# The first projection block worked in two halves of tokens, with its split weights kept in other buffers

## The chip, the cores and the metric

The kernel runs on one core of a Trainium2 chip. The metric is the device time of one execution in microseconds (us). The engines are named as in the profile: PE is the matrix engine, PEld its weight loads, DVE the vector engine, ACT the scalar engine, POOL the third one, SP the engine that issues most of the loads (its queue is SPq).

## The reference

One decoder layer over 512 tokens of width 2048. An RMS norm of x, one wide input projection, two token mixers fed from slices of that projection (an mLSTM and a gated delta rule), an output projection, a gated merge, and a last norm:

```python
D_MODEL = 2048; SEQ = 512
def _hybrid_layer(h, norm_w, w_in, ...):
    u = _rmsnorm(h, norm_w)                    # 512 x 2048
    proj = jnp.matmul(u, w_in.astype(jnp.float32))
    (ml_q, ml_k, ml_v, ml_o, ml_z, ml_i, ml_f,
     dn_qkv, dn_z, dn_b, dn_a, gate_a, gate_b) = jnp.split(proj, idx, axis=-1)
    h_a = mlstm(ml_q, ml_k, ml_v, ml_i, ml_f) ...
    h_b = gated_delta(dn_qkv, dn_b, dn_a) ...
    return jax.nn.sigmoid(gate_a) * (h_a @ w_out[:2048]) + jax.nn.sigmoid(gate_b) * (h_b @ w_out[2048:])
```

The change touches only the norm of x and the first 256 columns of the projection (a quarter of those of ml_q), with what runs beside them.

## The kernel before, in words

All matrices are f32. To multiply them at the faster rate of a reduced format, each operand is split into a high part (a cast to that format, `split_hi`, L135, on ACT) and a low part (the difference, `split_lo`, L138, on DVE); a product is then three matmuls: high by high, high by low, low by high (L261 to L263).

The start of the program runs like this. x lies as four tiles of 128 tokens by 2048 (`xts`), each loaded in two halves of 1024 columns by SP (L274). For each tile, ACT sums the squares of the first half (L301) and DVE those of the second (L303); two tiny operations and a power on POOL (L305, L306, L308) give the factor of each token; `scale_x` scales the first half on DVE (L294) and the second on ACT (L296). Then `make_u(kt)` makes slice kt (of 16) of the normalised input, tokens along the free axis: PE transposes the four tiles' 128 columns into one PSUM tile `put` (L317), ACT writes the high part `uh` (L318, times the norm weights `normc`), DVE the low part `ul` (L319).

The projection's weights come in pieces of 256 rows by 256 columns (two slices of k) in an order fixed by the list `plan`: `load_raw` issues a load on SP (L176) into one of four buffers `wr`, `split_next` splits it into `wh` and `wl` (four buffers each), and `prepare` keeps raw loads four pieces ahead and splits three ahead of the piece in use. A raw buffer comes free when its low part is written.

The first block, `proj_cm(ML_Q, before=first_block)`, runs over the 16 slices, two to a weight piece. Before a piece's products stand the transposes for the slices two ahead (UA = 2), and for later slices the products of the small gate columns (`gate_products`, L328 and L329, into `pgr`, eight slices behind). The products of one piece are 2 x 2 x 3 = 12 matmuls, each with a 128 x 128 weight part as the stationary operand and 512 tokens as the moving one. `first_block` also issues the loads of the gate columns (`wg`, two pieces, L333 and L334) and of small parameters, splits `wg` into `wgp`, and turns the convolution taps (`turn_taps`).

Behind the block come three more such blocks of q and k, then the main part, which works by sums of operand halves. Those sums are kept, split, in two large buffers `suh` and `sul` (L241); `u_sums` (L372 on) writes them once the first block is over:

```python
suh, sul = (sap.tile([P, KH, 3, HP], F32R, tag=f"su{n}", name=f"su{n}") for n in "hl")
```

KH is 8 and HP is 256. PE's instructions stand in the order in which they are written; those of the other engines are put in order by a scheduler, with hints of priority (`tc.high_priority`) and of place (`tc.issue_after`, `behind`). `tick()` moves side work on by one step.

Of the kernel before, what the change touches and what calls it, by code (L numbers as in the profile page):

```python
# [8 lines left out]
F32 = mybir.dt.float32  # L9
F32R = mybir.dt.float32r  # L10
AF = mybir.ActivationFunctionType
ALU = mybir.AluOpType
# [3 lines left out]
P = 128  # L16
# [39 lines left out]
def hybrid_body(  # L56
# [42 lines left out]
    def load_norms(tp, psp):  # L99
        nr = tp.tile([16, P], F32, tag="prow", name="nrow")  # L100
        nc.sync.dma_start(nr, norm_w.rearrange("(a p) -> a p", p=P))
        pt = psp.tile([P, 16], F32, tag="wk", name="pprm")
        T.transpose(pt, nr, ident[0:16, 0:16])
        V.tensor_copy(normc[:, 0:16], pt)

    def load_params(tp):
        nr = tp.tile([17, P], F32, tag="prow2", name="nrow2")
        nc.sync.dma_start(nr[0:16, :], ml_norm_w.rearrange("(a p) -> a p", p=P))
        nc.sync.dma_start(nr[16:17, :], dn_norm_w.rearrange("(a p) -> a p", p=P))
        cv = dn_conv_w.rearrange("j (a p) -> (j a) p", p=P)  # L110
# [29 lines left out]
    def behind(eng):  # L140

        return tc.issue_after(newest[eng])
# [17 lines left out]
    def load_raw():  # L160
        kind, c, k = plan[len(raws)]
        if kind == "m":

            qk = w_in[k * P:(k + KP) * P, ML_Q:ML_V].rearrange("(k p) (a n) -> p k a n", p=P, a=2)[:, :, :, c * P:(c + 1) * P]
            src, nk, n = None, KP, NB
        elif kind == "i":
            src, nk, n = w_in[k * P:(k + KP) * P, c:c + NB], KP, NB
        else:
            src, nk, n = w_out[k * P:(k + 1) * P, c:c + NO], 1, NO
        with tc.high_priority(offset=2 * PRIO if len(raws) > RAHEAD else 0):  # L170
            raw = wp.tile([P, nk, n], F32, tag="wr", name="wr", bufs=NRAW)
            if src is None:
                for i in range(KP):
                    nc.sync.dma_start(raw[:, i, :].rearrange("p (a n) -> p a n", a=2), qk[:, i])
            else:
                newest["S"] = nc.sync.dma_start(raw, src.rearrange("(k p) n -> p k n", p=P)).ins  # L176
        raws.append((raw, nk, n))

    def split_next():
        raw, nk, n = raws[len(parts)]  # L180
        with tc.high_priority(offset=2 * PRIO if len(parts) > SAHEAD else 0):
            hi = wp.tile([P, nk, n], F32R, tag="wh", name="wh", bufs=NSPL)
            lo = wp.tile([P, nk, n], F32R, tag="wl", name="wl", bufs=NSPL)
# [63 lines left out]

    banks = (((psj, "pj"),) * 3 + ((psw, "wk"),), ((psw, "wk"),) * 2 + ((pso, "o"),) * 2)

    def proj_cm(col0, before=None, kind="i"):  # L250
        ps = [psj.tile([P, S], F32, tag="pj", name="pj") for _ in range(2)]
        for kt0 in range(0, KT, KP):
            hi, lo = next_w(kind, col0, kt0)
            if before is not None:
                for k in range(KP):
                    before(kt0 + k)
            for j in range(2):
                for k in range(KP):
                    kt = kt0 + k
                    wsl = slice(j * P, (j + 1) * P)  # L260
                    T.matmul(ps[j], hi[:, k, wsl], uh[:, kt, :], start=(kt == 0), stop=False)  # L261
                    T.matmul(ps[j], hi[:, k, wsl], ul[:, kt, :], start=False, stop=False)  # L262
                    T.matmul(ps[j], lo[:, k, wsl], uh[:, kt, :], start=False, stop=(kt == KT - 1))  # L263
                tick()
        return ps
# [2 lines left out]
    p0 = p0s.enter_context(tc.tile_pool(name="p0", bufs=1))  # L268
    HD = D // 2
    xts = []  # L270
    for c in range(NC):
        xt = p0.tile([P, D], F32, tag=f"x{c}", name=f"xt{c}")
        for i in range(2):
            nc.sync.dma_start(xt[:, i * HD:(i + 1) * HD], x[c * P:(c + 1) * P, i * HD:(i + 1) * HD])  # L274
        xts.append(xt)
    for _ in range(2):
        load_raw()
    load_norms(p0, psw)
    wg = p0.tile([P, KT, 48], F32, tag="wg", name="wg")
    wgp = p0.tile([P, KT, 112], F32R, tag="wgp", name="wgp")  # L280
    wgh, wgl = wgp[:, :, 0:48], wgp[:, :, 64:112]
    G.memset(wgp[:, :, 48:64].bitcast(F32), 0.0)
    taps = []
# [8 lines left out]
    def scale_x(c):  # L292
        with tc.issue_after(sq["V"]):
            newest["V"] = V.tensor_scalar(out=xts[c][:, 0:HD], in0=xts[c][:, 0:HD], scalar1=rs[:, c:c + 1], scalar2=None,  # L294
                                        op0=ALU.mult).ins
        newest["A"] = A.mul(xts[c][:, HD:D], xts[c][:, HD:D], rs[:, c:c + 1]).ins  # L296

    for c in range(NC):
        xt = xts[c]
        jk = p0.tile([P, HD], F32, tag="jk", name="jk", bufs=2)  # L300
        A.activation(jk, xt[:, 0:HD], AF.Square, accum_out=ss[:, c, 0:1])  # L301
        jv = p0.tile([P, HD], F32, tag="jv", name="jv", bufs=2)
        sq["V"] = V.scalar_tensor_tensor(out=jv, in0=xt[:, HD:D], scalar=1.0, in1=xt[:, HD:D], op0=ALU.mult, op1=ALU.mult,  # L303
                                         accum_out=ss[:, c, 1:2]).ins
        V.tensor_tensor(out=rs[:, c:c + 1], in0=ss[:, c, 0:1], in1=ss[:, c, 1:2], op=ALU.add)  # L305
        V.tensor_scalar(out=rs[:, c:c + 1], in0=rs[:, c:c + 1], scalar1=1.0 / D, scalar2=EPS,  # L306
                        op0=ALU.mult, op1=ALU.add)
        G.tensor_tensor(out=rs[:, c:c + 1], in0=rs[:, c:c + 1], in1=mhalf[:, c:c + 1], op=ALU.pow)  # L308
        if c:
            scale_x(c - 1)  # L310
    scale_x(NC - 1)

    def make_u(kt):
        pool, tg = ((psw, "wk"), (pso, "o"))[kt % 2]
        pt = pool.tile([P, S], F32, tag=tg, name="put")
        for c in range(NC):
            T.transpose(pt[:, c * P:(c + 1) * P], xts[c][:, kt * P:(kt + 1) * P], ident)  # L317
        done["A"] = A.activation(uh[:, kt, :], pt, AF.Copy, scale=normc[:, kt:kt + 1]).ins  # L318
        done["V"] = V.scalar_tensor_tensor(out=ul[:, kt, :], in0=pt, scalar=normc[:, kt:kt + 1],  # L319
                                           in1=uh[:, kt, :].bitcast(F32), op0=ALU.mult, op1=ALU.subtract).ins  # L320

    UA = 2
    for kt in range(UA):
        make_u(kt)
    pgr = psw.tile([P, S], F32, tag="wk", name="pgr")

    def gate_products(kt):
        T.matmul(pgr[0:112, :], wgp[:, kt, :], uh[:, kt, :], start=(kt == 0), stop=False, skip_group_check=True)  # L328
        T.matmul(pgr[0:48, :], wgh[:, kt, :], ul[:, kt, :], start=False, stop=(kt == KT - 1), skip_group_check=True)  # L329

    def first_block(kt):
        if kt == 1:
            nc.sync.dma_start(wg[:, :, 0:16], w_in[:, ML_I:ML_I + 16].rearrange("(k p) n -> p k n", p=P))  # L333
            nc.sync.dma_start(wg[:, :, 16:48], w_in[:, DN_B:DN_B + 32].rearrange("(k p) n -> p k n", p=P))  # L334
        if kt == 3:
            taps.extend(load_params(p0))
        if kt == 6:
# [4 lines left out]
        if kt == 12:  # L342
            turn_taps(*taps, psw)
        if kt + UA < KT:
            make_u(kt + UA)
        if kt >= GLAG:
            gate_products(kt - GLAG)

    def spill(ps, o, scale):
        for j in range(2):  # L350
# [2 lines left out]
                A.mul(t, ps[j], scale)  # L353
                nc.scalar.dma_start(qk_d[o + j], t)

    ps = proj_cm(ML_Q, before=first_block)
    for kt in range(KT - GLAG, KT):
        gate_products(kt)
    gr0 = wp.tile([112, S], F32, tag="tg", name="gr0", bufs=3)
# [1287 lines left out]
```

## Time and profile before

| | |
|---|---|
| median of 3 runs | 2235.78 us (2233.39 to 2241.74) |
| the profiled execution | 2233.9 us, span 2232.1 us |
| PE busy | 2159.3 us, 97% |
| DVE busy | 1671.0 us, 75% |
| ACT busy | 995.0 us, 45% |
| DMA | 435.81 MB, mean 195 GB/s |
| PE busy from 0 to 18 us | 1.34 us |

Read it from the first line of the page down: the span is what the profiler saw of one execution, the execution's own time is 1.8 us more. Busy times are sums over the whole span; the views by stretch and the timeline tell when an engine was busy. A row of the timeline has the start, the length, the engine, the line and the operation (output, inputs, shape), how many were merged, and in brackets the idle time before and what ended it.

### The profile page before, as it was taken

The page shows a single profiled execution, that of the slowest core. Times are in us where ns is not written, and L with a number is a line of the kernel's source. Part 1 is how long each engine was busy: PE and PEld are TensorE (multiplying, and loading weights), DVE is VectorE, ACT ScalarE, POOL GpSimd, SP SyncE. Part 2 cuts the span into 40 slices and gives each one's busy share as a digit, 9 for nine tenths or more (in the row PEclk, how much of TensorE's full clock was granted, in tenths as well). Part 3 has the DMA queues.
Part 4 walks back from the last instruction along what each step waited for, and adds up shares of the span by engine and source line. Part 5 has one row for each costly group of instructions (what it writes and reads, how often), then busy time and mean ns, then how long its engine had stood idle before and what let it go on. Part 6 is the DMA issues. An engine that isn't in the chain of part 4 may idle for free. (4 is left out here: it accounts for less than half of the span.)

```text
span 2232.1 us, 31548 instructions
## 1 busy us (share of the span) xinstructions
PE 2159.3 (97%) x10592; PEld 1771.9 (79%) x10592; DVE 1671.0 (75%) x2907; ACT 995.0 (45%) x1890; POOL 276.6 (12%) x356
## 2 busy tenths in 40 slices
PE   7999999999999999999999999999999999999997
PEld 5877878888788788788878887878888887877775
DVE  5787788888878777877588876757675868667875
ACT  5444444444444343444544544444444445344344
POOL 0320000000000000000222422222222211110101
PEclk9999999999999999999999999999999999999999
DMA  5456666667667766776776767676756568695896
GB/s 156 125 174 193 199 201 201 205 202 231 197 208 228 235 210 205 229 244 192 195 189 168 179 145 174 147 172 166 178 139 167 141 153 230 186 278 184 250 317 215
DMA packets 534821, 435.81 MB, mean 195 GB/s; under 512 B 241921, under 2 KB 393698, under 8 KB 534530
## 3 DMA queue, kind: packets, MB, share of 16 engines
q1 hardware_dynamic: 425058, 357.68, 56.4%
q10 hardware_dynamic: 105568, 68.77, 9.8%
q0 software_dynamic: 4032, 7.34, 2.2%
q8 instruction: 83, 1.36, 0.3%
q14 instruction: 80, 0.66, 0.1%
HBM read 342.37 MB, written 95.49 MB: 196 GB/s over the span
## 5 line engine op out<-in xcount | busy, mean ns | idle before, releaser
L135 ACT CAST wh<-wr 128x512 fp32r<-128x512 f32 (+1 forms) x538 | 379.9, 707 | 470.9 <-PE pj L262 261.8
L138 DVE TENSOR_TENSOR wl<-wr,wh 128x512 fp32r<-128x512 f32 (+1 forms) x538 | 447.2, 834 | 178.2 <-ACT wh L135 160.2
L261 PE MATMUL pj<-uh,wh 128*128 128x512 f32 x1024 | 431.6, 421 | 4.2 <-ACT yp L770 4.2
L263 PE MATMUL pj<-uh,wl 128*128 128x512 f32 x1024 | 404.3, 395 | 0.0
L262 PE MATMUL pj<-ul,wh 128*128 128x512 f32 x1024 | 403.2, 394 | 0.0
L576 PE MATMUL ps<-wl,uh 128*128 128x512 f32 x704 | 277.3, 394 | 7.2 <-DVE wl L138 7.0
L575 PE MATMUL ps<-wh,uh 128*128 128x512 f32 x704 | 276.3, 392 | 7.0 <-DVE X L617 6.5
L577 PE MATMUL ps<-wh,ul 128*128 128x512 f32 x704 | 275.0, 391 | 0.0
L135 ACT CAST wh<-ts 128x512 fp32r<-128x512 f32 x224 | 138.2, 617 | 256.3 <-DVE ts L535 192.2
L135 ACT CAST wh<-t 128x1024 fp32r<-128x1024 f32 x112 | 117.9, 1053 | 250.9 <-PE ps L577 122.8
L263 PEld LDWEIGHTS pj<-uh,wl 128*128 128x128 f32 x1024 | 194.1, 190 | 43.3
L261 PEld LDWEIGHTS pj<-uh,wh 128*128 128x128 f32 x1024 | 195.2, 191 | 40.8 <-ACT yp L770 5.4
L576 PE MATMUL ps<-wl,suh 128*128 128x512 f32 x576 | 224.2, 389 | 1.6 <-DVE wl L138 1.6
L575 PE MATMUL ps<-wh,suh 128*128 128x512 f32 x576 | 224.5, 390 | 0.8 <-ACT qk L353 0.3
L577 PE MATMUL ps<-wh,sul 128*128 128x512 f32 x576 | 224.1, 389 | 0.0
L262 PEld LDWEIGHTS pj<-ul,wh 128*128 128x128 f32 x1024 | 195.6, 191 | 33.4
L138 DVE TENSOR_TENSOR wl<-ts,wh 128x512 fp32r<-128x512 f32 x224 | 153.6, 689 | 38.0 <-ACT wh L135 38.0
L138 DVE TENSOR_TENSOR wl<-t,wh 128x1024 fp32r<-128x1024 f32 x112 | 137.6, 1229 | 48.0 <-ACT wh L135 47.4
L576 PEld LDWEIGHTS ps<-wl,uh 128*128 128x128 f32 x704 | 132.6, 188 | 43.1 <-DVE wl L138 16.7
L575 PEld LDWEIGHTS ps<-wh,uh 128*128 128x128 f32 x704 | 132.5, 188 | 40.5 <-DVE X L617 12.7
L577 PEld LDWEIGHTS ps<-wh,ul 128*128 128x128 f32 x704 | 132.5, 188 | 26.7
L535 DVE TENSOR_TENSOR ts<-wr 128x512 f32<-128x512 f32 x112 | 77.2, 690 | 99.8 <-DMA wr<-t_d 76.0
(302 smaller groups left out, 3462.5 us busy)
## 6 DMA issues: line engine op xcount, KB each, us to landing
wr<-in_w_in_dram SPq DMA_DIRECT2D x704, 256.0 KB, 3.7
wr<-in_w_out_dram SPq DMA_DIRECT2D x138, 256.0 KB, 4.8
t_d<-ts ACTq DMA_DIRECT2D x96, 256.0 KB, 4.4
wr<-t_d SPq DMA_DIRECT2D x96, 256.0 KB, 4.1
wr<-in_w_in_dram SPq DMA_DIRECT2D x64, 128.0 KB, 3.2
xt<-in_x_dram SPq DMA_DIRECT2D x8, 512.0 KB, 7.2
tg_d<-X ACTq DMA_DIRECT2D x16, 256.0 KB, 6.1
tg_d<-to ACTq DMA_DIRECT2D x16, 256.0 KB, 5.1
```

The costliest lines, as they stand in the source:

```text
L135: newest["A"] = A.copy(hi, src).ins
L138: newest["V"] = V.tensor_tensor(out=lo, in0=src, in1=hi.bitcast(F32), op=ALU.subtract).ins
L261: T.matmul(ps[j], hi[:, k, wsl], uh[:, kt, :], start=(kt == 0), stop=False)
L262: T.matmul(ps[j], hi[:, k, wsl], ul[:, kt, :], start=False, stop=False)
L263: T.matmul(ps[j], lo[:, k, wsl], uh[:, kt, :], start=False, stop=(kt == KT - 1))
L535: V.tensor_tensor(out=ts[:, 0, :], in0=r[:, 0, :], in1=r[:, 2, :], op=ALU.subtract)
L575: T.matmul(ps[t], ah, hi, start=(g == "A" and i == 0), stop=False, skip_group_check=True)
L576: T.matmul(ps[t], ah, lo, start=False, stop=False, skip_group_check=True)
L577: T.matmul(ps[t], al, hi, start=False, stop=(i == KH - 1), skip_group_check=True)
```

## The change

Four things are done. The four x tiles are no longer handled together: the first block's 16 slices are worked twice, first for tokens 0 to 255 (x tiles 0 and 1), then for tokens 256 to 511, so that a step (h, kt) has two transposes, one half-width `uh` and `ul`, and six matmuls of 256 tokens. The block's eight split weight pieces must live for both halves: they are written into `suh` and `sul`, slot by slot, instead of into the rotating `wh` and `wl`. The loads of the first weight pieces stand between those of the third and fourth x tile. And the side work (`beside`) is placed anew by step number: statistics of the third tile at step 3 and of the fourth at 7, their scaling at 5 and 9, the loads of `wg` at 8 and of the parameters at 14, the split of `wg` at 19, the taps at 28. The gate products stand in the second half. The weight pieces of the block are all taken in the first half.

```diff
     def split_next():
         raw, nk, n = raws[len(parts)]
         with tc.high_priority(offset=2 * PRIO if len(parts) > SAHEAD else 0):
-            hi = wp.tile([P, nk, n], F32R, tag="wh", name="wh", bufs=NSPL)
-            lo = wp.tile([P, nk, n], F32R, tag="wl", name="wl", bufs=NSPL)
+            if len(parts) < KH:
+                hi, lo = (t[:, len(parts), 0:KP, :] for t in (suh, sul))
+            else:
+                hi = wp.tile([P, nk, n], F32R, tag="wh", name="wh", bufs=NSPL)
+                lo = wp.tile([P, nk, n], F32R, tag="wl", name="wl", bufs=NSPL)
...
+    for c in range(2):
         for i in range(2):
-            nc.sync.dma_start(xt[:, i * HD:(i + 1) * HD], x[c * P:(c + 1) * P, i * HD:(i + 1) * HD])
-        xts.append(xt)
-    for _ in range(2):
+            load_x(c, i)
+    load_norms(p0, psw)
+    load_raw()
+    load_raw()
+    for i in range(2):
+        load_x(2, i)
         load_raw()
-    load_norms(p0, psw)
+    for i in range(2):
+        load_x(3, i)
...
+    def make_u(kt, h):
         pool, tg = ((psw, "wk"), (pso, "o"))[kt % 2]
-        pt = pool.tile([P, S], F32, tag=tg, name="put")
-        for c in range(NC):
-            T.transpose(pt[:, c * P:(c + 1) * P], xts[c][:, kt * P:(kt + 1) * P], ident)
-        done["A"] = A.activation(uh[:, kt, :], pt, AF.Copy, scale=normc[:, kt:kt + 1]).ins
+        pt = pool.tile([P, HP], F32, tag=tg, name="put")
+        hs = slice(h * HP, (h + 1) * HP)
+        for c in range(2):
+            T.transpose(pt[:, c * P:(c + 1) * P], xts[2 * h + c][:, kt * P:(kt + 1) * P], ident)
+        done["A"] = A.activation(uh[:, kt, hs], pt, AF.Copy, scale=normc[:, kt:kt + 1]).ins
...
+    def beside(n):
+        if n in (3, 7):
+            stats(2 + n // 5)
+        if n in (5, 9):
+            scale_x(2 + n // 9)
+        if n == 8:
+            with behind("S"):
+                nc.sync.dma_start(wg[:, :, 0:16], w_in[:, ML_I:ML_I + 16].rearrange("(k p) n -> p k n", p=P))
+                nc.sync.dma_start(wg[:, :, 16:48], w_in[:, DN_B:DN_B + 32].rearrange("(k p) n -> p k n", p=P))
...
+    for n, (h, kt) in enumerate(steps):
+        if n < KT and n % KP == 0:
+            ws.append(next_w("i", ML_Q, kt))
+        beside(n)
+        if n + UA < len(steps):
+            make_u(steps[n + UA][1], steps[n + UA][0])
+        if n >= KT + GLAG:
             gate_products(kt - GLAG)
+        hi, lo = ws[kt // KP]
+        hs = slice(h * HP, (h + 1) * HP)
+        for j in range(2):
+            w = [t[:, kt % KP, j * P:(j + 1) * P] for t in (hi, lo)]
+            T.matmul(ps[j][:, hs], w[0], uh[:, kt, hs], start=(kt == 0), stop=False, skip_group_check=True)
+            T.matmul(ps[j][:, hs], w[0], ul[:, kt, hs], start=False, stop=False, skip_group_check=True)
+            T.matmul(ps[j][:, hs], w[1], uh[:, kt, hs], start=False, stop=(kt == KT - 1), skip_group_check=True)
+        if n % 2:
+            tick()
...
-    ps = proj_cm(ML_Q, before=first_block)
```

More of the change, by code (lines that the diff above doesn't have):

```diff
@@ L248, in hybrid_body, with proj_cm @@
     banks = (((psj, "pj"),) * 3 + ((psw, "wk"),), ((psw, "wk"),) * 2 + ((pso, "o"),) * 2)
-    def proj_cm(col0, before=None, kind="i"):
+    def proj_cm(col0, kind="i"):
         ps = [psj.tile([P, S], F32, tag="pj", name="pj") for _ in range(2)]
@@ L253, in proj_cm @@
             hi, lo = next_w(kind, col0, kt0)
-            if before is not None:
-                for k in range(KP):
-                    before(kt0 + k)
             for j in range(2):
@@ L270, in hybrid_body, with load_x @@
     xts = []
+    def load_x(c, i):
+        nc.sync.dma_start(xts[c][:, i * HD:(i + 1) * HD], x[c * P:(c + 1) * P, i * HD:(i + 1) * HD])
     for c in range(NC):
-        xt = p0.tile([P, D], F32, tag=f"x{c}", name=f"xt{c}")
+        xts.append(p0.tile([P, D], F32, tag=f"x{c}", name=f"xt{c}"))
+    for c in range(2):
         for i in range(2):
-            nc.sync.dma_start(xt[:, i * HD:(i + 1) * HD], x[c * P:(c + 1) * P, i * HD:(i + 1) * HD])
-        xts.append(xt)
-    for _ in range(2):
+            load_x(c, i)
[4 more added lines that the diff above has]
+        load_x(2, i)
         load_raw()
-    load_norms(p0, psw)
+    for i in range(2):
+        load_x(3, i)
     wg = p0.tile([P, KT, 48], F32, tag="wg", name="wg")
@@ L282, in hybrid_body @@
     G.memset(wgp[:, :, 48:64].bitcast(F32), 0.0)
-    taps = []
     ss = p0.tile([P, NC, 2], F32, tag="ss", name="ss")
@@ L296, in scale_x, with stats @@
         newest["A"] = A.mul(xts[c][:, HD:D], xts[c][:, HD:D], rs[:, c:c + 1]).ins
-    for c in range(NC):
+    def stats(c):
         xt = xts[c]
@@ L308, in hybrid_body @@
         G.tensor_tensor(out=rs[:, c:c + 1], in0=rs[:, c:c + 1], in1=mhalf[:, c:c + 1], op=ALU.pow)
[L309 to L313, printed above, removed]
+    def make_u(kt, h):
         pool, tg = ((psw, "wk"), (pso, "o"))[kt % 2]
-        pt = pool.tile([P, S], F32, tag=tg, name="put")
-        for c in range(NC):
-            T.transpose(pt[:, c * P:(c + 1) * P], xts[c][:, kt * P:(kt + 1) * P], ident)
-        done["A"] = A.activation(uh[:, kt, :], pt, AF.Copy, scale=normc[:, kt:kt + 1]).ins
[L319 to L325, printed above, removed]
+        pt = pool.tile([P, HP], F32, tag=tg, name="put")
[3 more added lines that the diff above has]
+        done["A"] = A.activation(uh[:, kt, hs], pt, AF.Copy, scale=normc[:, kt:kt + 1]).ins
+        done["V"] = V.scalar_tensor_tensor(out=ul[:, kt, hs], in0=pt, scalar=normc[:, kt:kt + 1],
+                                           in1=uh[:, kt, hs].bitcast(F32), op0=ALU.mult, op1=ALU.subtract).ins
     def gate_products(kt):
@@ L329, in gate_products @@
         T.matmul(pgr[0:48, :], wgh[:, kt, :], ul[:, kt, :], start=False, stop=(kt == KT - 1), skip_group_check=True)
[L331 to L337, printed above, removed]
+    UA = 2
+    steps = [(h, kt) for h in range(2) for kt in range(KT)]
+    taps = []
+    def beside(n):
[7 more added lines that the diff above has]
+                nc.sync.dma_start(wg[:, :, 16:48], w_in[:, DN_B:DN_B + 32].rearrange("(k p) n -> p k n", p=P))
+        if n == 14:
+            with behind("S"):
+                taps.extend(load_params(p0))
+        if n == 19:
             with tc.issue_after(done["A"]):
@@ L341, in first_block @@
                 split_lo(wgl, wg, wgh)
-        if kt == 12:
+        if n == 28:
             turn_taps(*taps, psw)
-        if kt + UA < KT:
-            make_u(kt + UA)
-        if kt >= GLAG:
-            gate_products(kt - GLAG)
+    stats(0)
+    stats(1)
+    scale_x(0)
+    scale_x(1)
+    for n in range(UA):
+        make_u(n, 0)
+    ps = [psj.tile([P, S], F32, tag="pj", name="pj") for _ in range(2)]
+    pgr = psw.tile([P, S], F32, tag="wk", name="pgr")
+    ws = []
+    for n, (h, kt) in enumerate(steps):
[5 more added lines that the diff above has]
+        if n >= KT + GLAG:
+            gate_products(kt - GLAG)
+        hi, lo = ws[kt // KP]
[7 more added lines that the diff above has]
+            tick()
     def spill(ps, o, scale):
```

## The prediction

> **What bounds the kernel now.** I read the page's busy times and slices first, then the busy time by stretches, then the timeline of the first 60 us, then groups of instructions by form.
>
> ```profile
> span 2232.1 us, 31548 instructions
> PE 2159.3 (97%) x10592; PEld 1771.9 (79%) x10592; DVE 1671.0 (75%) x2907; ACT 995.0 (45%) x1890; POOL 276.6 (12%) x356
> PE   7999999999999999999999999999999999999997
> ```
>
> The matrix engine (PE) sets the time: 97% busy, and its idle time is 2232.1 - 2159.3 = 73 us in all. The stretches tell where the change can reach it:
>
> ```profile
> 0.00:13.00 13.00, 0.00 (x0) 0.00 (x0) 4.91 (x12) 6.64 (x9) 2.18 (x12) 1.00 0.87 311
> 13.00:18.00 5.00, 1.34 (x4) 0.65 (x4) 3.83 (x10) 3.27 (x5) 1.10 (x2) 1.00 1.01 276
> 18.00:57.00 39.00, 38.99 (x191) 31.53 (x192) 20.60 (x32) 18.30 (x30) 0.00 (x0) 1.00 0.35 90
> 57.00:120.00 63.00, 63.00 (x295) 51.83 (x294) 49.13 (x82) 26.88 (x51) 24.46 (x26) 1.00 0.44 136
> ```
>
> The columns are length, busy PE, weight loads, DVE (VectorE), ACT (ScalarE), POOL, clock, DMA share and GB/s. PE does next to nothing for 18 us while x comes in (DMA at 0.87 to 1.01 of its engines); then it never rests until 120 us, through the first block (18 to 57) and beyond. In the first block DVE is busy for 20.6 of 39 us and ACT for 18.3: both wait for PE. The change is confined to the stretch up to 57 us, and what it wins or loses there passes on one to one, since PE is busy throughout the next 63 us and, apart from a few interleaved parameter loads, no engine's order changes behind the block.
>
> The timeline dates the start:
>
> ```profile
> 9.31 1.23 DVE L303 SCALAR_TENSOR_TENSOR jv<-xt 128x1024 f32<-128x1024 f32 x1 [1.92 <-DMA xt<-in_x_dram]
> 11.54 0.56 POOL L308 TENSOR_TENSOR rs<-rs,mhalf 128x1 f32<-128x1 f32 x1 [3.45 <-DVE rs L306]
> 11.75 0.37 SPq L333 DMA_DIRECT2D wg<-in_w_in_dram  x1
> 12.99 3.88 SPq L334 DMA_DIRECT2D wg<-in_w_in_dram  x1
> 14.29 1.23 DVE L303 SCALAR_TENSOR_TENSOR jv<-xt 128x1024 f32<-128x1024 f32 x1 [0.38 <-DMA xt<-in_x_dram]
> 17.20 0.76 DVE L294 TENSOR_SCALAR xt<-xt,rs 128x1024 f32<-128x1024 f32 x1 [0.66 <-POOL rs L308]
> 18.01 3.03 PE L317 MATMUL put<-ident,xt 128*128 128x128 f32 x13 [1.28 <-DVE xt L294]
> 20.69 0.78 PE L261 MATMUL pj<-uh,wh 128*128 128x512 f32 x1
> 20.81 1.89 DVE L138 TENSOR_TENSOR wl<-wr,wh 128x512 fp32r<-128x512 f32 x3
> 22.97 0.63 PE L263 MATMUL pj<-uh,wl 128*128 128x512 f32 x1
> 24.28 0.39 PE L261 MATMUL pj<-uh,wh 128*128 128x512 f32 x1
> 24.51 0.39 PE L262 MATMUL pj<-ul,wh 128*128 128x512 f32 x1
> 24.96 1.03 PE L317 MATMUL put<-ident,xt 128*128 128x128 f32 x8
> 26.07 0.39 PE L262 MATMUL pj<-ul,wh 128*128 128x512 f32 x1
> ```
>
> The second half of the second x tile is there at 9.31, that of the fourth at 14.29: 4.98/4 = 1.25 us for 512 KB, so 0.62 us for a weight load of 256 KB. The fourth tile is scaled at 17.20, and PE starts in earnest at 18.01. A warm 512-wide product takes 24.51 - 24.28 = 0.23 us.
>
> **Part 1, the earlier start: up to 5.2 us.** The second tile's factor is ready at 11.54 + 0.56 = 12.1 us. The change scales it then (0.75 us) and needs only two tiles for the first transposes, so PE can begin at 12.85 instead of 18.01.
>
> **Part 2, the products.** 96 of 512 columns become 192 of 256, and each brings its own weight load. No product with split operands runs 256 wide before. The nearest rows:
>
> ```profile
> 1096.05 0.60 PE L1117 MATMUL pnum<-v,wm 128*128 128x257 f32 x2
> 1096.49 1.05 PE L841 MATMUL pk<-kq 128*128 128x128 f32 x8
> 1097.62 0.39 PE L262 MATMUL pj<-ul,wh 128*128 128x512 f32 x1
> ```
>
> Eight plain-f32 products and one of 512 lie between 1096.49 and 1097.62, so one of the eight takes (1.13 - 0.23)/8 = 0.113 us, with a 128-column weight load for each. The eight transposes at 24.96 give (26.07 - 24.96 - 0.23)/8 = 0.11. So a weight load every 0.113 us does fit beside products. The upper end is the 257-wide pair: 0.44/2 = 0.22 us, hardly less than at 512. That pair has plain f32 operands, which cost 0.22/257 = 0.86 ns a column; the split kind costs 0.23/512 = 0.44 ns. The nearer row is that of the same kind, so I take 0.113: 192 x 0.113 = 21.7 us against 96 x 0.226 = 21.7, no change. The upper end is a rival below.
>
> **Part 3, the first half is not PE's any more.** One step of the new loop is two transposes and six products: 2 x 0.11 + 6 x 0.113 = 0.90 us of PE, and a step needs its slice of u from ACT and DVE. In the first half these must also do every weight split, the statistics and the scaling of tiles three and four. DVE's order, before, from the end of scaling:
>
> ```order
> L294 TENSOR_SCALAR xt3_115<-xt3_115,rs_131 128x1024
> L138 TENSOR_TENSOR wl_196<-wr_118,wh_195 128x512
> L319 SCALAR_TENSOR_TENSOR ul_88<-put_172,normc_82,uh_87 128x512
> L319 SCALAR_TENSOR_TENSOR ul_88<-put_179,normc_82,uh_87 128x512
> L138 TENSOR_TENSOR wl_200<-wr_120,wh_199 128x512
> L138 TENSOR_TENSOR wl_204<-wr_189,wh_203 128x512
> L138 TENSOR_TENSOR wl_208<-wr_191,wh_207 128x512
> ```
>
> and now, from the first weight split on:
>
> ```order
> L138 TENSOR_TENSOR sul_93<-wr_119,suh_92 128x512
> L325 SCALAR_TENSOR_TENSOR ul_88<-put_158,normc_82,uh_87 128x256
> L313 TENSOR_TENSOR rs_135<-ss_134 128x1
> L325 SCALAR_TENSOR_TENSOR ul_88<-put_163,normc_82,uh_87 128x256
> L138 TENSOR_TENSOR sul_93<-wr_121,suh_92 128x512
> L325 SCALAR_TENSOR_TENSOR ul_88<-put_181,normc_82,uh_87 128x256
> L314 TENSOR_SCALAR rs_135<-rs_135 128x1
> L138 TENSOR_TENSOR sul_93<-wr_124,suh_92 128x512
> L138 TENSOR_TENSOR sul_93<-wr_127,suh_92 128x512
> L311 SCALAR_TENSOR_TENSOR jv_281,ss_134<-xt3_109 128x1024
> L302 TENSOR_SCALAR xt2_108<-xt2_108,rs_135 128x1024
> L325 SCALAR_TENSOR_TENSOR ul_88<-put_192,normc_82,uh_87 128x256
> ```
>
> The fourth slice of u stands behind four splits, the fourth tile's statistics and the third tile's scaling. The third tile's statistics stand ahead of the first split. Counted on, twelve weight splits stand ahead of the twelfth slice, the last four of them for the next block. Their costs:
>
> ```profile
> L138 DVE TENSOR_TENSOR wl<-wr,wh 128x512 fp32r<-128x512 f32 x12 | 8.1, 690 | 13.4 <-ACT wh L135 11.3 <-PE put L317 2.2
> L135 ACT CAST wh<-wr 128x512 fp32r<-128x512 f32 x12 | 7.2, 618 | 16.5 <-PE pj L262 13.3 <-PE put L317 3.2
> L303 DVE SCALAR_TENSOR_TENSOR jv<-xt 128x1024 f32<-128x1024 f32 x4 | 4.9, 1226 | 8.3 <-DMA xt<-in_x_dram 8.3
> L294 DVE TENSOR_SCALAR xt<-xt,rs 128x1024 f32<-128x1024 f32 x4 | 3.0, 751 | 0.7 <-POOL rs L308 0.7
> L1129 DVE SCALAR_TENSOR_TENSOR c<-c,de,pcs 128x257 f32<-128x257 f32 x16 | 7.7, 479 | 9.3 <-PE pcs L1123 9.3
> L1133 ACT COPY v<-pnum 128x257 f32<-128x257 f32 x32 | 12.0, 374 | 43.2 <-PE pcs L1123 29.2 <-DMA tt<-xd 7.6 <-DMA h_d<-to 4.3
> L296 ACT ACTIVATE xt<-xt,rs 128x1024 f32<-128x1024 f32 x4 | 4.6, 1144 | 2.1 <-POOL rs L308 2.1
> L301 ACT ACTIVATE jk<-xt 128x1024 f32<-128x1024 f32 x4 | 4.2, 1053 | 5.3 <-DMA xt<-in_x_dram 5.3
> ```
>
> No half-width slice of u runs before; L1129 (257 columns, read from PSUM, the same operation) prices DVE's part, L1133 ACT's. DVE's work up to the twelfth slice: 2 x 1.226 + 2 x 0.751 + 12 x 0.690 + 12 x 0.479 + four tiny ones at about 0.15 = 18.6 us. Back to back it is less: three splits take 1.89 instead of 2.07 (row at 20.81), 0.09 saved each, 2.5 us over some 28 instructions, so 16.1 at least. ACT's up to there: two statistics, three scalings, twelve casts, twelve slices: 2.1 + 3.4 + 7.4 + 4.5 = 17.4 us, about as much, so the two also wait for one another. DVE starts on it when the third tile is there: 9.31 + two weight loads + two x halves, 9.31 + 1.24 + 2.5 = 13.1 us. The twelfth slice is ready between 13.1 + 16.1 = 29.2 and 13.1 + 18.6 = 31.7.
>
> **Part 4, the loads that feed it.** What SP's queue has, before, from the last x tile to wg:
>
> ```order
> L274 DMA xt3_115<-in_x_dram 128x1024 x2
> L101 DMA nrow_122<-in_norm_w_dram 16x128
> L176 DMA wr_118<-in_w_in_dram 128x2x256
> L176 DMA wr_120<-in_w_in_dram 128x2x256
> L176 DMA wr_189<-in_w_in_dram 128x2x256
> L176 DMA wr_191<-in_w_in_dram 128x2x256
> L333 DMA wg_127<-in_w_in_dram 128x16x16
> L334 DMA wg_127<-in_w_in_dram 128x16x32
> ```
>
> and now, from the fourth weight load on:
>
> ```order
> L176 DMA wr_127<-in_w_in_dram 128x2x256
> L273 DMA xt3_109<-in_x_dram 128x1024
> L176 DMA wr_171<-in_w_in_dram 128x2x256
> L176 DMA wr_203<-in_w_in_dram 128x2x256
> L176 DMA wr_236<-in_w_in_dram 128x2x256
> L176 DMA wr_264<-in_w_in_dram 128x2x256
> L176 DMA wr_297<-in_w_in_dram 128x2x256
> L343 DMA wg_131<-in_w_in_dram 128x16x16
> L176 DMA wr_327<-in_w_in_dram 128x2x256
> L344 DMA wg_131<-in_w_in_dram 128x16x32
> L176 DMA wr_355<-in_w_in_dram 128x2x256
> L176 DMA wr_383<-in_w_in_dram 128x2x256
> ```
>
> From the fifth on, a load waits for the split that frees its buffer (four buffers). The second wg piece now stands ahead of the eleventh and twelfth loads, whose casts stand ahead of the eleventh and twelfth slices on ACT. Issuing a wg piece took 0.37 us once and 3.88 once (rows above). At 0.37 it costs nothing. At 3.88 from about 22.9 us (after the sixth split) the eleventh load leaves at 26.8, lands 3.7 later
>
> ```profile
> wr<-in_w_in_dram SPq DMA_DIRECT2D x704, 256.0 KB, 3.7
> ```
>
> at 30.5, and two casts (0.62 each) and the slice (0.37 + 0.48) put the twelfth slice at about 32.6 to 33. So it comes between 29.2 and 33; I take 31.2, in the upper part, since both engines must also wait for loads.
>
> **The sum.** From the twelfth slice PE has five steps of the first half, 5 x 0.90 = 4.5 us: it ends at 35.7. The second half needs no splits, 0.37 us of ACT and 0.48 of DVE a step against 0.90 of PE: PE-bound. Its work: 16 x 0.90 = 14.4, sixteen pairs of gate products and the taps.
>
> ```profile
> 44.67 0.39 PE L263 MATMUL pj<-uh,wl 128*128 128x512 f32 x1
> 45.38 0.60 PE L317 MATMUL put<-ident,xt 128*128 128x128 f32 x4
> 53.57 0.40 PE L328 MATMUL pgr<-uh,wgp 128*112 128x512 f32 x1
> 57.27 0.40 PE L261 MATMUL pj<-uh,wh 128*128 128x512 f32 x1
> ```
>
> Eight pairs take 57.27 - 53.57 = 3.7 us, so all 7.4; the taps 45.38 - 44.67 - 0.23 = 0.5. In all 22.3, and the second block starts at 35.7 + 22.3 = 58.0 instead of 57.27: +0.7 us, with 29.2 and 33 giving -1.3 and +2.5. The 5.2 us of earlier start are given back as waits of PE for DVE and ACT. The profiled execution took 2233.9 us, 1.9 under the median of 2235.78; the sum is 2234.6 against it and 2236.5 against the median. I forecast 2236.
>
> **The rivals.**
>
> The early start is kept: PE, not DVE, paces the first half, and the second block starts 5.2 us earlier: 2233.9 - 5.2 = 2228.7. For it: DVE's busy share in the first block is 20.6/39. Against: the 16.1 us that must precede the twelfth slice, from 13.1 on. 9%.
>
> PE stays at half speed. The rows at 20.69 to 22.97 show 0.63 us where 0.39 is the later duration, for about 3 us after the products began, though the clock column reads 1.00. In the new first half PE has gaps; if they keep it slow, a step costs 6 x 0.225 + 2 x 0.23 = 1.8 us, sixteen from about 15.4 (13.1, the third tile's statistics, a split and a slice) end at 44.2 instead of 35.7: 58.0 + 8.5 = 66.5, +9.2, so 2243 (2245 by the median). Against: DVE's pace leaves PE at least two thirds busy. 10%. The Trainium skill, "TensorE: Matmul & The Clock Gate", Part 1, says that the array runs at half clock until about 3.4 us of sustained activity and falls back after an idle window of that length. By that rule the slow phase here would end as soon as it does before, and this rival would need a gap of 3.4 us; the trace agrees on the 3 us of warming up and shows no such gap to test the rest.
>
> Slower: the weight load is not hidden at 256 columns. Place: all 192 products; price: 0.226 each as at 512. A first-half step is then 6 x 0.226 + 0.22 = 1.58, sixteen end at 15.4 + 25.3 = 40.7, and the second half is 96 x 0.113 = 10.8 longer: 40.7 + 33.1 = 73.8, +16.5, so 2250 (2252 by the median). It decides from about 0.20 us a product, where the loss passes 0.5% (11.2 us). For it: the 257-wide pair, and weight loads of 0.19 us that start only as the product before them starts. Against: the loads at 0.113. 6%.
>
> The change misses its aim: second half or next block waits for the load queue, where small parameter loads now stand between weight loads. Four split pairs for the next block are ready beforehand, so up to 2 us: within the forecast.
>
> **The numbers.** Forecast 75%, rivals 9, 10 and 6. 0.5% (11.2 us) is about what a measurement of this kernel can tell from no change; the forecast, the early start and the half clock all stay inside it. Slower 0.07: the third rival and a little of the second; faster 0.02; within 0.91. The range goes from 2230 (the forecast's low end of 2232.6, and part of the first rival) to 2245 (half clock, by the median), leaving out the third rival and the rest.
>
> **What would show it.** Transposes from about 12.9 us; products of 256 columns 0.113 us apart where PE doesn't wait; PE idle some 4 to 6 us between 15 and 33, put down to DVE's ul or ACT's uh; the second half without waits at 0.90 us a step; the second block starting at 57 to 60 us. Wrong if it starts before 55 or after 62, or if PE is idle for under 2 us in the first half.

## The result, and the profile after

The kernel after takes 2242.06 us (median of 13 executions, 2240.23 to 2248.73), the kernel before in the same session 2232.95 (13 executions, 2226.53 to 2241.74). The ratio is 1.0045 with a 95% interval of 1.0033 to 1.0057: some 9 to 10 us slower, less than the 0.5% that the prediction took as its bound for no change, but clearly not nothing. The profiled execution took 2244.32 us, that of the kernel before 2233.9; the traces compared below are these two. The head of its page:

```profile
span 2242.5 us, 31767 instructions
PE 2168.4 (97%) x10688; PEld 1781.6 (79%) x10688; DVE 1674.9 (75%) x2923; ACT 997.1 (44%) x1906; POOL 276.5 (12%) x356
```

PE has 96 products and 96 weight loads more. Its lines have moved: the new first block is L377 to L379 with transposes in L323 and u in L324 and L325; what stood behind the block has 33 added to its number. The start in stretches, with the columns of the stretches before:

```profile
0.00:13.00 13.00, 0.73 (x2) 0.36 (x2) 4.39 (x11) 6.23 (x9) 2.17 (x12) 1.00 0.86 301
13.00:20.00 7.00, 6.35 (x27) 5.66 (x27) 6.66 (x15) 7.00 (x14) 0.93 (x1) 1.00 0.90 294
20.00:30.00 10.00, 8.66 (x60) 7.45 (x59) 7.80 (x18) 6.68 (x14) 0.93 (x1) 1.00 0.85 185
57.00:120.00 63.00, 63.00 (x295) 51.53 (x294) 46.66 (x81) 26.76 (x51) 23.98 (x26) 1.00 0.44 135
```

PE starts five microseconds earlier, works from 13 us on, and has small gaps from 20 to 30. The timeline shows at what pace, and where the block ends:

```profile
13.17 1.33 PE L323 MATMUL put<-ident,xt 128*128 128x128 f32 x5 [1.29 <-DVE xt L302]
15.56 0.58 PE L378 MATMUL pj<-ul,suh 128*128 128x256 f32 x1 [0.47 <-DVE ul L325]
15.94 0.41 PE L379 MATMUL pj<-uh,sul 128*128 128x256 f32 x1
16.15 0.41 PE L377 MATMUL pj<-uh,suh 128*128 128x256 f32 x1
21.09 0.28 PE L377 MATMUL pj<-uh,suh 128*128 128x256 f32 x1
21.21 0.28 PE L378 MATMUL pj<-ul,suh 128*128 128x256 f32 x1
34.55 0.38 PE L323 MATMUL put<-ident,xt 128*128 128x128 f32 x2
35.49 0.38 PE L323 MATMUL put<-ident,xt 128*128 128x128 f32 x2
36.42 0.38 PE L323 MATMUL put<-ident,xt 128*128 128x128 f32 x2
58.78 0.40 PE L261 MATMUL pj<-uh,wh 128*128 128x512 f32 x1
```

Until about 20.5 us the products are 0.21 us apart, then 0.12; a step takes 0.93 to 0.94 us (34.55 to 35.49 to 36.42). The second block starts at 58.78 instead of 57.27: 1.5 us late. That is all that the first block loses; the time is longer by 10.

The place for the rest is found by following the same piece of work through both timelines. After, the eight plain products that stood at 1096.49 us before:

```profile
1096.72 1.05 PE L874 MATMUL pk<-kq 128*128 128x128 f32 x8
```

Of the 1.5 us only 0.2 are left: PE waits for 9.1 us between 120 and 1090 where it waited for 11.5. The loss appears afterwards, in the stretch in which the two mixers run beside the remaining projections. Waits of PE from 1300 to 2030 us, before and then after (engine, line, what for, total, times, longest):

```profile
PE p L966 <- ACT s L962: 7.8, 4, 2.6
PE pr L990 <- DVE st L1009: 2.4, 1, 2.4
PE py L1307 <- DVE wl L138: 2.3, 3, 1.3
PE py L1306 <- ACT wh L135: 2.0, 1, 2.0
```

```profile
PE p L999 <- ACT s L995: 13.0, 5, 4.0
PE py L1340 <- DVE wl L138: 3.9, 2, 3.5
PE py L1339 <- ACT wh L135: 3.1, 1, 3.1
PE pr L1023 <- DVE st L1042: 1.2, 1, 1.2
```

All rows of these two answers add up to 19.4 us before and 26.3 after: 6.9 us of the loss are waits. The rest is PE running slower. The view by windows over the same 3969 products, first before, then after (length, busy PE, and in the third column from the end the clock):

```profile
1300.00:2030.00 730.00, 710.56 (x3969) 590.09 (x3968) 513.39 (x1197) 315.34 (x775) 152.60 (x193) 0.99 0.70 177
1300.67:2042.26 741.59, 715.27 (x3969) 593.73 (x3968) 514.57 (x1197) 315.26 (x777) 152.16 (x193) 0.98 0.69 174
```

The same products keep PE busy for 4.7 us longer. The clock records show why: at half clock are 13.7 us of this stretch before and 23.9 after, and half of the difference, 5.1 us, is about that. The 6.9 us of waits and the 4.7 make up the 11.6 us by which the stretch is longer. The change touches no instruction there: the order of the operations behind the block is the same.

### The profile page after: what moved, and what is told of

Its sections match the earlier page's. It is cut to its first block, busy times and chain, and to the rows that moved or that the text cites. A ratio compares the mean times of both kernels' runs of the same rounds, so it can differ in the third digit from the quotient of the medians.

```text
span 2242.5 us, 31767 instructions
## 1 busy us (share of the span) xinstructions
PE 2168.4 (97%) x10688; PEld 1781.6 (79%) x10688; DVE 1674.9 (75%) x2923; ACT 997.1 (44%) x1906; POOL 276.5 (12%) x356
## 3 DMA queue, kind: packets, MB, share of 16 engines
q8 instruction: 83, 1.36, 0.3%
## 5 line engine op out<-in xcount | busy, mean ns | idle before, releaser
L135 ACT CAST wh<-wr 128x512 fp32r<-128x512 f32 (+1 forms) x530 | 374.8, 708 | 455.5 <-PE pj L262 251.2
L261 PE MATMUL pj<-uh,wh 128*128 128x512 f32 x992 | 418.1, 421 | 3.5 <-ACT yp L803 3.5
L263 PE MATMUL pj<-uh,wl 128*128 128x512 f32 x992 | 390.6, 394 | 0.0
L262 PE MATMUL pj<-ul,wh 128*128 128x512 f32 x992 | 390.3, 393 | 0.0
L263 PEld LDWEIGHTS pj<-uh,wl 128*128 128x128 f32 x992 | 188.0, 189 | 41.9
L261 PEld LDWEIGHTS pj<-uh,wh 128*128 128x128 f32 x992 | 188.5, 190 | 38.7 <-ACT yp L803 4.8
L262 PEld LDWEIGHTS pj<-ul,wh 128*128 128x128 f32 x992 | 189.0, 190 | 32.0
```

The lines of the kernel that those rows point to most:

```text
L135: newest["A"] = A.copy(hi, src).ins
```

## The experiments

What is seen to differ 1300 us behind the first block is a short list: the block starts 1.5 us later; three PSUM tiles have changed places; PE's, ACT's and DVE's programs have become longer by 191, 11 and 18 records. Each experiment gives the kernel before one of these, or takes one from the kernel after. All ratios are to the kernel before on the same chip in the same session.

**Another place in PSUM.** To the kernel before, one transpose more, which turns the rotation of the PSUM tiles:

```diff
         if kt == 6:
+            for _ in range(1):
+                T.transpose(pgr[:, 0:P], ident, ident)
```

> The kernel before with one added 128-column transpose early in the first block, which only serves to make the allocator hand the three rotating PSUM banks (wk) round in another order for the rest of the program; no engine's order changes behind the block. If the 8 us that the change lost behind the first block come from which PSUM bank a tile lies in: 2238 to 2243. If they come from time carried over from the first block, or from the longer code of PE: 2233, as the kernel before. If any small change in timing moves the time by several us: somewhere from 2228 to 2243.

2236.16 us against 2235.69, ratio 1.0000 [0.9984, 1.0015]. The counterpart, two 16-column transposes in the kernel after that give its tiles another permutation:

> The changed kernel with two added 16-column transposes around the gate products, which make the allocator hand the three rotating PSUM banks round in another order. If the banks are the cause: 2233 to 2235. If the first block's time or the code's length is: 2242. If small changes in timing move the time: somewhere from 2233 to 2248.

2244.45 us, 1.0044 [1.0028, 1.006], as without them. The PSUM places are not the cause.

**A later second block.** The kernel before with 14 transposes behind the first block, so that the second starts 1.6 us later:

```diff
+    for _ in range(2):
+        pd = psw.tile([P, S], F32, tag="wk", name="pd")
+        for _ in range(7):
+            T.transpose(pd[:, 0:P], ident, ident)
     spill(ps, 0, float(P) ** -0.5)
```

> The kernel before with 14 added 128-column transposes into unused PSUM tiles at the end of the first block: the second block starts about 1.5 us later (58.8 us instead of 57.3), as it does in the changed kernel (58.6); PSUM banks and two small SBUF buffers change places. If lost time in the first block is passed on one to one: 2234.5. If the main part makes it up: 2233. If the time behind the block depends on where its waits fall: up to 2243, with more half-clock windows of PE and longer waits for the small products at about 1370 to 1700 and 1980 to 2010 us.

2237.65 us, 1.0005 [0.9988, 1.0022]. A shift of this size costs 1 us, with an interval from -3 to 5: about half of the 10 us, or more, must come from elsewhere.

**Work ahead of the start.** 96 transposes of 128 columns on PE before x is there:

```diff
+    for _ in range(2):
+        pd = pso.tile([P, S], F32, tag="o", name="pd")
+        for _ in range(48):
+            T.transpose(pd[:, 0:P], ident, ident)
     xts = []
```

> The kernel before with 96 added 128-column transposes at the very start, where PE waits for x: as many matmuls more as in the changed kernel, all banks and addresses as before. If the longer code of PE costs time later: 2239 to 2241. If not, and transposes bring PE to full clock: the products at 20.7 us run at full speed and the second block starts some 2.5 us earlier (54.8), 2230.5 if that is passed on. If transposes don't bring the clock up: 2233.

2239.9 us, 1.0019 [1.0002, 1.0035]. It was meant to save the slow products at the start, and it does:

```profile
1.64 13.18 PE L273 MATMUL pd<-ident 128*128 128x128 f32 x96 [1.64 <-POOL half L293]
20.43 0.40 PE L263 MATMUL pj<-uh,wl 128*128 128x512 f32 x1
20.67 0.39 PE L261 MATMUL pj<-uh,wh 128*128 128x512 f32 x1
```

(0.39 instead of 0.63 us). Yet the kernel is slower by 4 us. What it shares with the kernel after is some 192 more records in PE's program (a product or transpose and its weight load are two), and this pointed to how the program reaches the engine. The queues of the page of before:

```profile
q8 instruction: 83, 1.36, 0.3%
q14 instruction: 80, 0.66, 0.1%
```

1.36 MB in 83 packets are 16,384 bytes each; PE has 10,657 records on its queue and 10,592 of products, 21,249 in all, so a packet holds 256 of them. The packets of q14 have 8,192 bytes; by their number they serve the other engines, which have 10,299 records, about 129 to a packet. The Trainium skill, "Runtime: NRT & Kernel Launch", section "Instruction fetch mechanics", describes blocks of 16 KiB with 256 instructions, and calls the cost of crossing a boundary mostly hidden. The size agrees with the trace for PE and is half of that for the rest. If the position of the packets matters (theory F), 192 records are three quarters of a packet, so every later fetch falls on other work.

The traces show one such case from end to end. ACT's queue at the same work, before and after (start, length, queue, line, operation):

```profile
1360.07 0.72 ACTq L806 DMA_DIRECT2D hm_d<-to  x1
1361.05 0.60 ACT L135 CAST wh<-wr 128x512 fp32r<-128x512 f32 x1
1361.39 1.67 ACTq L806 DMA_DIRECT2D hm_d<-to  x2
1363.10 0.78 ACT L942 ACTIVATE s<-p 32x256 f32<-32x256 f32 x2 [1.45 <-DVE jd L846]
```

```profile
1360.06 0.73 ACTq L839 DMA_DIRECT2D hm_d<-to  x1
1361.04 0.60 ACT L135 CAST wh<-wr 128x512 fp32r<-128x512 f32 x1
1364.05 1.25 ACTq L839 DMA_DIRECT2D hm_d<-to  x2
1365.34 0.78 ACT L975 ACTIVATE s<-p 32x256 f32<-32x256 f32 x2 [3.70 <-DVE jd L879]
```

Up to 1361 us the two agree to 0.01 us. Then the fourth store waits 2.7 us longer, and `s` behind it 2.2. The store waits for the semaphore (the counter of what has landed) that a weight load uses, issued at 1358.33 and 1358.32; of that load's sixteen slices all had landed at 1361.36 before, while after fifteen were in at 1361.77 and the last at 1364.02. The view of the queues from 1359 to 1364 us has the packets (queue, count, MB, share) and the stores (count, size, median us from issue to landing), first before, then after:

```profile
hm_d<-to ACTq DMA_DIRECT2D x6, 64.0 KB, 4.1
```

```profile
q8 instruction: 1, 0.02, 2.5%
q14 instruction: 1, 0.01, 0.4%
...
hm_d<-to ACTq DMA_DIRECT2D x3, 64.0 KB, 7.0
```

Before there is no instruction packet in this stretch (PE's come at 1351.4 and 1367.4); after, one of PE's runs from 1360.4 to 1362.4. It coincides with the one late slice; whether both used the same DMA engine the trace doesn't name. This single case costs PE only 0.6 us, and shows a path: a fetch, a late slice, a store held, ACT's queue held, PE's wait for `s`.

The first step of this path is no single case. The traces record when each slice lands; five of the queues' semaphores have counts that divide into whole transfers of sixteen. Before, 55 of their transfers had their eighth slice land while one of PE's packets ran, and in 27 of these the last slice came over 1 us behind the fifteenth; of the other 1197 transfers, in 43. After, it is 21 of 63 against 54 of 1190. So a fetch for PE often goes with one late slice, and did so before the change. The late transfers are about as many, 70 and 75, but other ones: counted from the end of each semaphore, only 3 are late in both.

**The count alone, in four kernels.** One part of the change by itself, the products in halves in the old order:

```diff
+                    for h in ((slice(0, HP), slice(HP, S)) if before is not None else (slice(0, S),)):
+                        T.matmul(ps[j][:, h], hi[:, k, wsl], uh[:, kt, h], start=(kt == 0), stop=False, skip_group_check=before is not None)
...
```

(in this order the sums of the first block's 256 columns come out wrong, so this kernel only serves to measure time; its products and weight loads are as many and as large as in the kernel after), and tiny transposes ahead of everything, 2 x 48 or 2 x 64 in the kernel before, 2 x 16 in the kernel after:

```diff
+    for _ in range(2):
+        pd = pso.tile([P, S], F32, tag="o", name="pd")
+        for _ in range(48):
+            T.transpose(pd[:, 0:16], ident[0:16, :], ident[0:16, 0:16])
```

> The kernel before with one part of the change alone: the products of the first block run in two halves of 256 columns each, in the old order (192 more PE records), and nothing else. Theory F: the later fetches move as in the kernel after: 2240 to 2245, ratio 1.002 to 1.0045. Rival B: the halves by themselves cost at most the 0.5 us of the first block, which later waits absorb: 2234 to 2238, ratio 1.000.

> The kernel before with 96 transposes of 16 columns ahead of everything on PE (192 more PE records, done before PE's first work at 25.7 us); nothing else. Theory F: as the kernel after, 2240 to 2245, ratio 1.002 to 1.0045. Rival B: 2234 to 2238, ratio 1.000.

> The same with 128 transposes (256 more PE records, one whole packet). Theory F: the fetches stand where they stood: 2234 to 2238, ratio 1.000. A third theory W (work ahead of the start costs by itself, whatever its count, for instance because the clock is then raised earlier): both padded kernels come out alike, 2238 to 2242. Rival B: 2234 to 2238 for both.

> The kernel after, with 32 transposes of 16 columns put ahead of everything on PE (64 more PE instructions with their weight loads; PE is idle there until 11.4 us anyway). Theory F (place of the instruction fetches): PE's program comes in packets of 16,384 bytes, 83 in the kernel before for 21,249 PE records, so 256 records each; the change puts 191 records ahead of the second block, and a fetch that took 1.0 us at 1351.4 now comes at 1360.4, takes 2.0 and holds up a slice of a load that ACT's queue waits for. 64 more make the shift 255, a whole packet: the fetches stand at the work where they stood before, and the time comes back to 2234 to 2239, a ratio to the kernel before of 1.000 (0.999 to 1.0015). Rival B (what is lost comes from the new first block itself, or from the other engines' programs, 11 ACT and 18 DVE records longer): 2242 to 2246, ratio 1.0045 as without the transposes.

Halves alone: 2241.07 us against 2235.7, 1.0031 [1.0015, 1.0047]. 96 transposes, done at 12.05 us and ahead of PE's first work at 15.83: 2241.16, 1.0026 [1.001, 1.0042]. 128: 2237.3, 1.0014 [1.0002, 1.0025]. The kernel after with 32: 2240.77, 1.0028 [1.0016, 1.004], where it had 1.0045.

Rival B, by which nothing outside the first block costs, is rejected: the old order with 192 more records, and even the old first block whole behind 96 transposes, are slower by 5.4 us. Theory F has the right side in all four, but not the right size in two: 128 transposes were to give 1.000, and the kernel after with 32 was to come back to 2239 at most. A whole packet gives back a part only. The intervals of 96 and 128 overlap, and so do those of the kernel after with 32 and without: that a whole packet costs less is likely and not shown, and the interval of 128 lies above 1, too. W, by which both would be alike, is not excluded by these two alone. The kernel after with 32 transposes no longer has the case above. Its ACT queue at the same work:

```profile
1361.19 0.74 ACTq L843 DMA_DIRECT2D hm_d<-to  x1
1362.15 0.60 ACT L135 CAST wh<-wr 128x512 fp32r<-128x512 f32 x1
1363.08 1.22 ACTq L843 DMA_DIRECT2D hm_d<-to  x2
1364.34 0.78 ACT L979 ACTIVATE s<-p 32x256 f32<-32x256 f32 x2 [1.59 <-DMA gz<-gz_d]
```

Between the third and the fourth store lie 1.9 us (1.3 before, 4.0 after), and PE's fetches stand around it at 1352.2 and 1368.3, nearly where they stood before the change. So the padding moves the fetches as theory F says.

**The other engines' programs, and another phase.**

```diff
+    scr = p0.tile([P, 32], F32, tag="scr", name="scr")
+    for i in range(11):
+        A.copy(scr[:, i:i + 1], ident[:, i:i + 1])
+    for i in range(11, 29):
+        V.tensor_copy(scr[:, i:i + 1], ident[:, i:i + 1])
```

> The kernel before with 11 one-column copies on ACT and 18 on DVE ahead of everything, where both engines are idle (the counts by which the change lengthens their programs); PE's program untouched. Theory F2 (the packets of 8,192 bytes, in which the programs of ACT, DVE, SP and POOL come, count too): slower by the 2 to 6 us that stayed in the kernel after when 32 transposes had put PE's fetches back, 2238 to 2242, ratio 1.001 to 1.003. Theory F1 (PE's fetches alone): 2234 to 2238, ratio 1.000.

> The kernel before with both paddings: 96 transposes on PE, 11 copies on ACT, 18 on DVE; the first block is the old one, whole. Theory F2: the whole loss of the kernel after without any of its change, 2242 to 2247, ratio 1.0035 to 1.0055. F1: as with 96 transposes alone, 2239 to 2243, ratio 1.0026. Rival B (the rest of the loss is the new first block's): also 1.0026.

> The kernel before with 64 transposes of 16 columns ahead of everything on PE (128 more PE records, half a packet). Theory F: a phase not seen yet, so its size is open, anywhere from 2228 to 2245; not bound to lie between none (2235.7) and 96 (2241.2). Theory W (padding costs by its count): between them, 2238 to 2240, and 128 transposes, at 2237.3 already below 96, speak against it.

ACT and DVE alone: 1.0013 [0.9994, 1.0032], which tells nothing between no cost and 7 us. With the 96 transposes besides: 2244.69 against 2238.88, 1.0025 [1.0008, 1.0042], the same as the transposes alone, so F2 found no support. 64 transposes: 2238.14 against 2238.88, 1.0002 [0.9986, 1.0018]. A cost by count (W) was to give 2238 to 2240 there for a kernel before at 2235.7, a ratio of 1.001 to 1.002, so this run speaks against W and doesn't exclude it.

**All of it together.** 82 tiny transposes ahead, 14 of 128 columns behind the first block, and the 29 copies:

> The kernel before with all that the trace shows of the change beyond its first block, and none of its code: 82 transposes of 16 columns ahead of everything on PE and 14 of 128 columns behind the last products of the first block (together the 192 records of the change, and a second block that starts 1.6 us later, where the kernel after starts it 1.5 us later), 11 copies on ACT and 18 on DVE ahead of everything. If the place of the fetches and the later start make up the loss between them: 2243 to 2248, ratio 1.0035 to 1.0055, as the kernel after. If only the records count: as with all three paddings without the late start, 1.001 to 1.004 about 1.0025, and then some 4 us of the loss stay without a cause.

2243.06 us against 2236.75, 1.0037 [1.0021, 1.0053]: within what the first reading expected, though the interval reaches down to the second. The kernel before, with its old first block and none of the change's code, then loses about as much as the change does.

By the records that the traces count more in PE's program the twelve kernels and the kernel after sort like this:

| records more on PE | ratios |
|---|---|
| 0 to 28 | 1.0013, 1.0000, 1.0005 |
| 127 | 1.0002 |
| 191 to 195 | 1.0019, 1.0025, 1.0026, 1.0031, 1.0037; with the change 1.0044, 1.0045 |
| 254, 255 | 1.0014; with the change 1.0028 |

Shown is that some 192 records on PE cost time, be they halves of products, large transposes or tiny ones: all five kernels that have them without the whole change are slower, each with an interval above 1, by 0.19 to 0.31% (4 to 7 us) where the second block isn't late. They cost it far behind the place where they stand. The eight plain products of 1096.49 us, in the profiled execution with 96 tiny transposes:

```profile
1095.55 1.05 PE L845 MATMUL pk<-kq 128*128 128x128 f32 x8
```

There this execution is 0.9 us ahead of the one before; its span of 2238.3 us ends 6.2 behind.

That they cost by where they put the fetches is the best reading and not shown: the fetches do move by the count, they go with late slices, one case is seen from end to end, and 64 and 128 transposes cost less by their point values. The late transfers move with the count, too: of the 70 of the kernel before, 34 are late again in the kernel with one record more, 15 with 128 tiny transposes and 3 with 96; with 96, 17 are those of the kernel after. By chance some 4 would agree (70 x 75/1252). But that one case isn't how the others lose time. From the first store to `s` pass 4.1 us before and 6.4 after, and only 4.4 to 4.7 in the five kernels with some 192 records. Which late slices lead to the larger waits was not traced in any kernel. Open is what in the kernel after adds the 0.15 to 0.2% by which it lies above the padded kernels; the later start and the longer programs of ACT and DVE were each too small to measure, and all together are within the interval.

## Why the prediction was right, and where it wasn't

**Part 1** held: the first transposes run at 11.40 and 13.17 us, forecast 12.85.

**Part 2** held: 0.12 us apart once the clock is up (21.09, 21.21; forecast 0.113). The slower rival at 0.226 is out. A step of 0.90 us became one of 0.93 to 0.94.

**Part 3** had the end nearly right and the reason partly wrong. The first half ends at about 36.4 us, forecast 35.7. PE was to be idle for 4 to 6 us, waiting for DVE and ACT. Its waits from the first product to the end of the first half:

```profile
PE pj L378 <- DVE ul L325: 1.5, 4, 0.5
PE pj L378 <- DVE rs L314: 0.5, 1, 0.5
PE pj L377 <- ACT uh L324: 0.4, 1, 0.4
```

2.4 us, so DVE and ACT do hold PE up, but about half as long as forecast, and little over the 2 us below which I would have called this part wrong. The other half of the head start went to products at half speed: from 14.5 to 20.5 us one takes 0.21 us instead of 0.12, 6.0 x 0.09/0.21 = 2.6 us. I had that as a rival for the whole first half; it holds for its first 6 us, and the forecast's own sum had no term for it.

**Part 4** and the sum held: no wait of PE for the load queue, and the second half took 58.78 - 36.4 = 22.4 us for a forecast of 22.3. The second block starts at +1.5 us, between the bounds of -1.3 and +2.5.

**What failed** is the sentence that what is won or lost up to 57 us "passes on one to one". It was argued from a busy PE up to 120 us, and only that far. Behind it PE waits for others, and the later start was absorbed there: 0.2 us were left at 1096 us, and the same shift alone measured 1.0005. A second effect, for which the sum had no term, then added most of the loss: the 192 records. Part 2 prices them at their time on PE, and there they cost next to nothing; they cost later, in PE's waits and the half-clock stretches among them, most likely by where they put the fetches. 2242 us is in the range and 6 above the forecast of 2236; against the kernel before of its own session the change costs 9 us where the sum had 0.7. That it lies in the range is luck: the upper end of 2245 was set for a first half wholly at half speed, not for a loss behind the block. So the first block was mostly understood, but not the way from there to the end.

## What to carry to other kernels

Adding instructions to PE's program need not be free behind the place where they stand, even if they run in idle time: 96 tiny transposes before the first work cost 0.26% here, while 64 cost nothing that could be measured. When a small edit at the start moves the end, follow one piece of work through both timelines to where they part, and try the bare count in the old kernel before explaining the edit. And a shift of the start passes on only as far as the bounding engine never waits.

## What was not expected of the hardware

PE's program comes during the run in packets of 16,384 bytes, and those looked at took 0.9 to 2.0 us. Transfers that land while one runs often have one slice over 1 us late: 27 of 55 in the kernel before, against 43 of the other 1197.

PE falls to half clock for a few microseconds after waits in the middle of the kernel. In the timeline of the kernel after, a wait of 3.34 us, and the products behind it 0.42 us apart instead of 0.23:

```profile
1692.96 1.88 PE L999 MATMUL p<-tb,s 64*64 64x64 f32 x16 [3.34 <-ACT s L995]
1697.07 0.63 PE L263 MATMUL pj<-uh,wl 128*128 128x512 f32 x1
1697.49 0.63 PE L261 MATMUL pj<-uh,wh 128*128 128x512 f32 x1
```

The same stretch in the view by windows, whose clock column (third from the end) reads 0.50 for 6.8 us, so that half of it, 3.4 us, is lost on top of the wait:

```profile
1693.10:1699.90 6.80, 6.80 (x28) 5.62 (x28) 5.41 (x9) 2.88 (x6) 0.83 (x1) 0.50 0.53 135
```

A wait as long as that isn't needed. The clock record of the kernel before has six stretches of 3.4 us at half clock ahead of its last products, and the longest wait in the 5 us ahead of each is 1.3 to 2.6 us, though not every such wait brings one. The gap of 3.4 us that the prediction names as needed for its rival of half speed is not needed here.

Transposes of 128 columns raise the clock like products do: in the kernel that began with 96 of them the clock record reads full from 6.8 us on, about 5 us after they began. The 96 transposes of 16 columns, in 10.4 us, did not: there the record starts at 23.3 us. The Trainium skill, "TensorE: Matmul & The Clock Gate", Part 4, says that transpose mode does not count as busy in the same way; here the measurement of the large ones says otherwise, if these f32 transposes run in that mode, which the trace doesn't name.
